# A macaron layer step in fp32: an inverse of corner blocks turned by TensorE in place of a round trip through DRAM, with sigmoid rewritten as tanh

## The chip, the cores and the metric

The kernel runs on one core of a Trainium2 chip. The metric is the device time of one execution in microseconds (us), the median of the runs. TensorE is PE in the profile (its weight loads are PEld), VectorE is DVE, ScalarE is ACT, GpSimd is POOL and SyncE is SP, which issues most DMAs.

## What is computed

One step of one layer, for 256 prompt tokens and 8 sample tokens, in fp32. The layer has three parts: a half-step SwiGLU FFN, mixing, and a second FFN, each behind an RMSNorm:

```python
x = x + FFN_RES * swiglu(rmsnorm(x, n1), f1g, f1u, f1d)
h = rmsnorm(x, nm)
proj = h @ w_in
...
o_att, k_buf, v_buf = attend(q, k, v, sinks)
o_rwkv, shift, S = rwkv_time_mix(proj[..., ATT_COLS:], ...)
mixed = jnp.concatenate([o_att, o_rwkv], axis=-1)
x = x + mixed @ w_out
x = x + FFN_RES * swiglu(rmsnorm(x, n2), f2g, f2u, f2d)
```

The change lies in `rwkv_time_mix` and, in two lines, in the softmax of the attention. For each head the state `S` (64 x 64) goes through the tokens:

```python
a = jax.nn.sigmoid(a0 + al @ a2)
g = jax.nn.sigmoid(gl) @ g2
kk = k * k_k
k = k * (1.0 + (a - 1.0) * k_a)
...
sa = einsum('bhij,bhj->bhi', S, -kk_t)
S = S * exp(lw_t)[:, :, None, :] + sa[..., None] * (kk_t * a_t)[:, :, None, :] + v_t[..., None] * k_t[:, :, None, :]
y_t = einsum('bhij,bhj->bhi', S, r_t)
```

## The kernel before

**Weights.** Every weight arrives from DRAM in pieces of 128 x 512 (`raw`, a ring of 6 buffers, issued by SP). ScalarE casts a piece to its high part (`hi`, line 123), VectorE subtracts for the low part (`lo`, through line 58), rings of 4 each. A piece makes twelve TensorE matmuls of 128 x 128 weights by 264 columns, three for each 128 x 128 block (`hi` with the two halves of x, `lo` with one), all recorded at line 74 as `acc<-s,hi` and `acc<-s,lo`. Both FFNs are little else.

**Mixing.** The input weights `win` (152 pieces) and the output weights `wout` go through the same path. After each piece `tick` lets every task, a Python generator, write one more stretch of its code, and `pause(n)` lets n pieces pass. The tasks are `prep` (one for each pair of heads, eight in all), `chain` (one for each batch of two pairs, four in all) and `attend` (one for each of eight query tiles). The scheduler of the language then puts the instructions of each engine in their final order, by a simulated timeline of its own. Each engine executes its queue in order.

**The chain of a batch.** RWKV runs in chunks of 64 tokens, four for each pair. `prep` computes the decay (`sg`, through sigmoid), `a`, the scaled keys `kr`, `bk`, and their masked products `gm` (`m<-kr,bk` on TensorE, the mask on VectorE). Each chunk needs the inverse of a triangular 64 x 64 matrix; its 32 x 32 corner blocks on the diagonal go by DMA to DRAM (`sa`) and return in two layouts, `X` and `Xt`, so that 128 partitions (4 column groups of 32 matrices) do the forward substitution: 30 steps on VectorE, each a product `st` and an addition to `Xt`. The result goes to DRAM once more (`sb`, line 544), returns as `TT` with a matrix to 32 partitions (line 549), VectorE adds the identity (line 556) and transposes (`TN`, line 559). From there: `TN,gm`, a copy `zs`, `TT,zs`, then `kr,TT`; the copies `W` (ScalarE) and `uv` (VectorE, line 596); `BT,W`, `gm,W`, `uv,BT`, `gm,uv`; `N` on VectorE; `N,PT` and the short chain over the four chunks; the group norm (`y,C`, `t,C`), the gate `sgl,ld`, and `mixed`, which the output weights take as their input.

`Xt`, `X`, `TN`, `zs` and `W` have one buffer, so the next batch's loads wait for the readers of this one. Small products use the five PSUM banks `m`, the big ones three `acc`. `DWAIT` and `PW` at the top of the file are the pauses.

Of the kernel before, what the change touches and what calls it, by code (L numbers as in the profile page):

```python
# [7 lines left out]
F32 = mybir.dt.float32  # L8
F32R = mybir.dt.float32r
AF = mybir.ActivationFunctionType  # L10
ALU = mybir.AluOpType
AX = mybir.AxisListType

P = 128
NP = 256
NB = 8
T = NP + NB
# [7 lines left out]
HALF = (slice(0, 64), slice(64, 128))  # L25
PARTS = [8, 7, 7, 7, 7, 7]
BATCH = [2, 2, 2, 2]
# [6 lines left out]
DWAIT = (8,8,8,4)  # L34
# [8 lines left out]
VMU, VKK, VKA, VA0, VRK, VLW, VLB, VSK, VSD = 64, 90, 98, 106, 114, 122, 130, 138, 154  # L43
# [4 lines left out]
def body(tc, I, O):  # L48
    nc = tc.nc
    V, A, G, TE, SP = nc.vector, nc.scalar, nc.gpsimd, nc.tensor, nc.sync  # L50
# [6 lines left out]
    def tt(e, out, a, b, op):  # L57
        return e.tensor_tensor(out=out, in0=a, in1=b, op=op)  # L58

    def stt(out, a, s, b, op0, op1):  # L60
        return V.scalar_tensor_tensor(out=out, in0=a, scalar=s, in1=b, op0=op0, op1=op1)  # L61

    def ts(e, out, a, s1, op0, s2=None, op1=None):
        k = {} if op1 is None else dict(op1=op1)
        e.tensor_scalar(out=out, in0=a, scalar1=s1, scalar2=s2, op0=op0, **k)

    def act(out, in_, f, **k):
        return A.activation(out=out, in_=in_, func=f, **k)  # L68

    def bc(ap, shape):  # L70
        return ap.broadcast_to(list(shape))

    def mm(out, lhsT, rhs, start=True, stop=True, **k):
        TE.matmul(out, lhsT, rhs, start=start, stop=stop, **k)  # L74
# [16 lines left out]
    def pause(n):  # L91
        for _ in range(n):
            yield

    with ExitStack() as ctx:
# [4 lines left out]
        dp = ctx.enter_context(tc.tile_pool(name="dp", bufs=1, space=bass.MemoryType.DRAM))  # L100
# [12 lines left out]
        def mp():  # L113
            return pp.tile([P, 512], F32, tag="m", bufs=NM, name=uid("m"))
# [28 lines left out]
        vec = cp.tile([P, NVEC], F32, name="vec")  # L143
# [13 lines left out]
        def vc(i):  # L157
            return vec[:, i:i + 1]
# [173 lines left out]
        def mixing_body(mx, n2, n3, XD):  # L332
            def fix(shape, name):
                return mx.tile(list(shape), F32, name=name)

            def ring(shape, tag, bufs):
                return mx.tile(list(shape), F32, tag=tag, bufs=bufs, name=uid(tag))
# [6 lines left out]
            ident, bo, cm = C[:, CID:CID + P], C[:, CBO:CBO + P], C[:, CCM:CCM + P]  # L344
# [7 lines left out]
            for pj in PJ:  # L352
                G.memset(pj[:, 0:1], 0.0)
            nmu = fix((P, NSH), "nmu")
            mu = vec[:, VMU:VMU + NSH]
            ts(V, nmu, mu, -1.0, ALU.mult, 1.0, ALU.add)
            tt(V, ss, ss, bc(mu.unsqueeze(2), (P, NSH, NB)), ALU.mult)
            qd = fix((P, 2, NB, 4), "qd")
            nbat = len(BATCH)
            scr = [dp.tile([BATCH[b] * 16, 1024], F32, tag=f"sa{b}", name=f"sa{b}") for b in range(nbat)]  # L360
            scr2 = [dp.tile([BATCH[b] * 16, 1024], F32, tag=f"sb{b}", name=f"sb{b}") for b in range(nbat)]
            mixed = [None] * 16
            have = [False]

# [19 lines left out]
            la, sgl = fix((P, T), "la"), fix((P, T), "sgl")  # L384
# [4 lines left out]
            def c4(x):  # L389
                return x[:, :NP].rearrange("p (c t) -> p c t", c=4)  # L390

            def prep(p, bt, k, xrr, xk, xv):
                lw = load(I["lw"][p], (P, 256))
                zp = mp()
# [3 lines left out]
                ap = mp()  # L398
                mm(ap[:, :T], lw[:, P:2 * P], la)
                sg, a = tmp(), tmp()  # L400
                act(sg, zp[:, :T], AF.Sigmoid)
                act(a, ap[:, :T], AF.Sigmoid, bias=vc(VA0 + p))
                kk, b = tmp(), tmp()
                act(kk, xk, AF.Copy, scale=vc(VKK + p))
                act(b, kk, AF.Square)
# [8 lines left out]
                W, Wi = tmp((P, 4, 65)), tmp((P, 4, 64))  # L414
# [5 lines left out]
                yield from pause(PW[1])  # L420
                rk = tmp((P, T + 2 * NB))
                stt(b, b, 1e24, kk, ALU.min, ALU.mult)
                tt(V, b, b, a, ALU.mult)
                ts(V, a, a, 1.0, ALU.subtract, vc(VKA + p), ALU.mult)
                kx = a
                stt(kx, a, 1.0, xk, ALU.add, ALU.mult)
                stt(rk[:, :T], xrr, vc(VRK + p), kx, ALU.mult, ALU.mult)
                yield
                BK, KR = ring((P, 4, 3, 64), "bk", 2), ring((P, 3, 4, 64), "kr", NKR)
                bt.KR[k] = KR  # L430
                stt(KR[:, 0], c4(kk), -1.0, W[:, :, 0:64], ALU.mult, ALU.mult)
                tt(V, KR[:, 1], c4(xrr), W[:, :, 1:65], ALU.mult)
                s4 = (P, 4, 2, 64)
                tt(V, BK[:, :, 0:3:2, :], bc(c4(b).unsqueeze(2), s4), bc(Wi.unsqueeze(2), s4), ALU.mult)
                tt(V, BK[:, :, 1, :], c4(kx), Wi, ALU.mult)
                for i, src in ((6, kk), (2, b), (3, xv), (4, kx), (5, xrr)):
                    G.tensor_copy(XD[:, i, p, :], src[:, NP:T])
                dq = rk[:, T:].rearrange("p (s b) -> p s b", s=2)
                tt(G, XD[:, 7, p, :], XD[:, 1, p, :], XD[:, 5, p, :], ALU.mult)
# [76 lines left out]
            def chain(bt):  # L516
# [24 lines left out]
                    if s % NSTEP == 0:  # L541
                        yield
                for g in range(ng):
                    SP.dma_start(scr2[bt.i].rearrange("r (j g t) -> g r j t", g=ng, t=32)[g], Y[g * nr:(g + 1) * nr])  # L544
                yield from pause(1)
                for h in range(2):
                    for blk in range(2):
                        x = h * 64 + blk * 32
                        SP.dma_start(TT[x:x + 32, :, blk * 32:blk * 32 + 32],
                                     scr2[bt.i].rearrange("(h b m) (s t) -> h b s m t", h=2, b=2, s=32)[h, blk])  # L550
                yield from pause(DWAIT[bt.i])
                for h in range(2):
                    for blk in range(2):
                        x = h * 64 + blk * 32
                        v = TT[x:x + 32, :, blk * 32:blk * 32 + 32]
                        tt(V, v, v, bc(ident[x:x + 32, x:x + 32].unsqueeze(1), (32, n * 4, 32)), ALU.add)
                TN = ring((P, n * 4, 32), "TN", 1)
                for h in range(2):
                    V.transpose(TN[h * 64:h * 64 + 32], TT[h * 64:h * 64 + 32, :, 0:32])
                yield  # L560
                ps = mp()
                for k in range(n):
# [29 lines left out]
                for k in range(n):  # L592
                    v = wus[k].rearrange("p (c t) -> p c t", c=4)
                    A.copy(W[:, k], v[:, 1:4, 0:64])
                    for h in range(2):
                        V.tensor_copy(uv[HALF[h], :, k, HALF[h]], v[HALF[h], :, 64:128])
                yield
                pbs = [mp() for _ in range(n)]
                for k in range(n):
# [101 lines left out]
            def softmax(s, mxv, sinks, n):  # L701
                nm, sm, es = (ring((P, 4), "st" + x, 6) for x in "abc")
                ts(V, nm[:, :n], mxv[:, :n], -1.0, ALU.mult)
                for j in range(n):
                    act(s[j], s[j], AF.Exp, bias=nm[:, j:j + 1], accum_out=sm[:, j:j + 1])
                w = n // len(sinks)
                for h, x in enumerate(sinks):
                    act(es[:, h * w:(h + 1) * w], nm[:, h * w:(h + 1) * w], AF.Exp, bias=x)
                tt(V, sm[:, :n], sm[:, :n], es[:, :n], ALU.add)
                V.reciprocal(sm[:, :n], sm[:, :n])  # L710
                for j in range(n):
                    ts(V, s[j], s[j], sm[:, j:j + 1], ALU.mult)

            def attend(t, q):
                p = t // 4
# [103 lines left out]
            shifted(0, la)  # L819
            act(tw[0:64, :], la[0:64, :], AF.Tanh)  # L820
            shifted(1, sgl)
            act(sgl, sgl, AF.Sigmoid)
            bat, att, bts = [], [], []
            for kind, i in SEQ:
                if kind == "b":
# [202 lines left out]
```

## Time and profile before

| | us |
|---|---|
| median of 3 runs | 2034.14 (2033.25 to 2035.09) |
| profiled execution | 2030.2, span 2028.1, clock 0.996 |
| mixing, by the trace | from about 796 to 1212 |
| TensorE busy in it | 396.25 of 416.50 |
| VectorE, ScalarE, POOL busy in it | 315.56, 233.94, 49.06 |

A row of the timeline has the start, the duration, the engine, the line, the operation, `out<-in`, shapes, and how many instructions it joins; the bracket is the engine's idle time before and what ended it. A window's row has, for each engine, its busy time in that stretch, then the granted clock, the DMA share and GB/s. An fp32 product shows as two matmul rows, so `x32` there is 16 products. A group's row has busy time and mean ns of one.

### The profile page before, as it was taken

How to read it: one execution, taken by the hardware profiler on the slowest of the kernel's cores; microseconds unless marked ns; L12 is line 12 of the kernel's file. 1: busy time of each engine (PE TensorE's matmuls, PEld its weight loads, DVE VectorE, ACT ScalarE, POOL GpSimd, SP SyncE). 2: the span in 40 equal slices, each digit the busy share in tenths (PEclk: the TensorE clock that was granted, in tenths of full speed). 3: DMA queues.
4: the chain of work that ended last, by engine and by line, in shares of the span. 5: the costliest groups of instructions: out<-in, count | busy, mean ns of one | idle time of the engine just before them, and what ended most of it. 6: DMA issues, size and time to landing. Idle time of an engine off the chain costs nothing.

```text
span 2028.1 us, 45390 instructions
## 1 busy us (share of the span) xinstructions
PE 1994.5 (98%) x17096; PEld 1956.8 (96%) x17096; DVE 1321.9 (65%) x2623; ACT 1035.2 (51%) x2027; POOL 240.9 (12%) x337
## 2 busy tenths in 40 slices
PE   9999999999999999999999899999999999999998
PEld 9999999999999999998898789999999999999998
DVE  5865555655556577678778766775666666666665
ACT  5644444444444466665555455554444444444445
POOL 0301001010110122111100010120101101010012
PEclk9999999999999999999999899999999999999999
DMA  6565655655556566554455345465566555655654
GB/s 226 178 187 196 184 193 188 185 185 176 186 170 192 181 207 204 155 159 121 134 148 166 91 133 185 171 184 178 191 181 195 180 192 189 187 191 180 195 181 145
DMA packets 227421, 358.38 MB, mean 177 GB/s; under 512 B 42353, under 2 KB 80769, under 8 KB 227201
## 3 DMA queue, kind: packets, MB, share of 16 engines
q1 hardware_dynamic: 220752, 346.95, 55.0%
q10 hardware_dynamic: 6448, 8.53, 1.3%
q8 instruction: 134, 2.20, 0.5%
q14 instruction: 87, 0.70, 0.1%
HBM read 347.25 MB, written 10.21 MB: 176 GB/s over the span
## 4 chain that ended last, share of the span: by engine, by line
PE 93%; DVE 3%; DMA 2%; ACT 1%; issue 1%; SPq 0%; ACTq 0%; DVEq 0%
PE acc L74 84%; PE m L74 7%; DVE lo L58 1%; DMA TT<-sb 1%; DMA sb<-Xt 0%; DMA raw<-in_win 0%; DVE y L58 0%; ACT t L68 0%; DVE t L678 0%; DMA raw<-in_gu 0%; DVE Xt L58 0%; DVE st L58 0%; ACT L68 0%; SPq L544 0%; DVE t L732 0%
## 5 line engine op out<-in xcount | busy, mean ns | idle before, releaser
L58 DVE TENSOR_TENSOR lo<-raw,hi 128x512 fp32r<-128x512 f32 (+1 forms) x1288 | 869.3, 679 | 546.4 <-ACT hi L123 518.5
L123 ACT CAST hi<-raw 128x512 fp32r<-128x512 f32 (+1 forms) x1288 | 775.9, 607 | 860.2 <-PE acc L74 777.6
L74 PE MATMUL acc<-s,hi 128*128 128x264 f32 x5940 | 1107.3, 286 | 4.7 <-ACT hi L123 2.5
L74 PEld LDWEIGHTS acc<-s,hi 128*128 128x128 f32 x5940 | 921.9, 188 | 10.3 <-issue 4.0
L74 PE MATMUL acc<-s,lo 128*128 128x264 f32 x2970 | 848.1, 286 | 5.3 <-DVE lo L58 5.3
L74 PEld LDWEIGHTS acc<-s,lo 128*128 128x128 f32 x2970 | 558.9, 188 | 8.8 <-DVE lo L58 6.6
L74 PE MATMUL acc<-t,hi 128*128 128x264 f32 x2752 | 503.0, 284 | 0.0
L74 PEld LDWEIGHTS acc<-t,hi 128*128 128x128 f32 x2752 | 426.3, 188 | 0.0
L74 PE MATMUL acc<-t,lo 128*128 128x264 f32 x1376 | 388.9, 285 | 0.0
L58 POOL TENSOR_TENSOR t<-t,t 128x264 f32<-128x264 f32 (+1 forms) x148 | 150.7, 1018 | 1151.2 <-ACT hi L123 791.0
L74 PEld LDWEIGHTS acc<-t,lo 128*128 128x128 f32 x1376 | 258.4, 188 | 0.1
L74 PE MATMUL acc<-y,hi 128*128 128x264 f32 x648 | 124.5, 284 | 0.0
L74 PEld LDWEIGHTS acc<-y,hi 128*128 128x128 f32 x648 | 101.8, 189 | 0.2
L74 PE MATMUL acc<-y,lo 128*128 128x264 f32 x324 | 92.5, 285 | 0.0
L58 DVE TENSOR_TENSOR t<-acc,t 128x264 f32<-128x264 f32 x156 | 67.4, 432 | 37.1 <-PE acc L74 36.9
L74 PE MATMUL acc<-o,hi 128*128 128x264 f32 x324 | 63.5, 286 | 0.0
L58 POOL TENSOR_TENSOR o<-o,o 128x264 f32<-128x264 f32 x43 | 35.9, 834 | 230.8 <-ACT o L68 225.1
L74 PEld LDWEIGHTS acc<-y,lo 128*128 128x128 f32 x324 | 60.8, 188 | 0.0
L61 DVE SCALAR_TENSOR_TENSOR s<-acc,s 128x264 f32<-128x264 f32 x96 | 40.6, 427 | 16.0 <-PE acc L74 15.5
L74 PEld LDWEIGHTS acc<-o,hi 128*128 128x128 f32 x324 | 50.3, 188 | 0.0
L74 PE MATMUL m<-s,hi 128*128 128x264 f32 x260 | 48.5, 285 | 0.0
L61 DVE SCALAR_TENSOR_TENSOR x<-acc,x 128x264 f32<-128x264 f32 x96 | 40.5, 427 | 10.0 <-PE acc L74 9.6
(236 smaller groups left out, 1288.7 us busy)
## 6 DMA issues: line engine op xcount, KB each, us to landing
raw<-in_gu SPq DMA_DIRECT2D x688, 256.0 KB, 3.3
raw<-in_dn SPq DMA_DIRECT2D x224, 256.0 KB, 2.8
raw<-in_win SPq DMA_DIRECT2D x152, 256.0 KB, 3.4
raw<-in_dn SPq DMA_DIRECT2D x160, 192.0 KB, 2.7
raw<-in_wout SPq DMA_DIRECT2D x64, 256.0 KB, 3.2
xsp<-x ACTq DMA_DIRECT2D x16, 132.0 KB, 3.2
s<-xsp SPq DMA_DIRECT2D x16, 132.0 KB, 4.2
ld<-in_sT SPq DMA_DIRECT2D x16, 128.0 KB, 3.2
```

What stands on the lines that cost most here:

```text
L58: return e.tensor_tensor(out=out, in0=a, in1=b, op=op)
L61: return V.scalar_tensor_tensor(out=out, in0=a, scalar=s, in1=b, op0=op0, op1=op1)
L74: TE.matmul(out, lhsT, rhs, start=start, stop=stop, **k)
L123: A.copy(hi[:, :w], raw[:, :w])
```

## The change

Four things are edited:

- The second trip through DRAM goes. POOL writes ones on the diagonal of `Xt`. 32 products with identity columns, `C,Xt`, bring the inverse on TensorE into one PSUM bank, 32 partitions for a matrix; ScalarE copies it to `TN`, and four VectorE transposes make `TT`. `TN,gm` reads the copy directly.
- Sigmoid becomes tanh of half the argument. Of `sg` and `sgl` POOL makes 0.5 t + 0.5; `a` stays a tanh, and its factor and offset go into the products that use it.
- Half of the `uv` copies, and two of four softmax scalings of an attention tile, go from VectorE to ScalarE.
- The pause behind the substitution is 8 pieces, in place of 1 and `DWAIT`.

```diff
+            half = fix((P, 16), "half")
+            ts(V, half, vec[:, VKA:VKA + 16], 0.5, ALU.mult)
+            less = fix((P, 8), "less")
+            ts(V, less, half[:, 0:8], -1.0, ALU.mult, 1.0, ALU.add)
...
-                act(sg, zp[:, :T], AF.Sigmoid)
-                act(a, ap[:, :T], AF.Sigmoid, bias=vc(VA0 + p))
+                act(sg, zp[:, :T], AF.Tanh, scale=0.5)
+                ts(G, sg, sg, 0.5, ALU.mult, 0.5, ALU.add)
+                act(a, ap[:, :T], AF.Tanh, scale=0.5, bias=half[:, 8 + p:9 + p])
...
-                tt(V, b, b, a, ALU.mult)
-                ts(V, a, a, 1.0, ALU.subtract, vc(VKA + p), ALU.mult)
+                stt(b, a, 1.0, b, ALU.add, ALU.mult)
+                act(a, a, AF.Identity, scale=half[:, p:p + 1], bias=less[:, p:p + 1])
                 kx = a
-                stt(kx, a, 1.0, xk, ALU.add, ALU.mult)
+                tt(V, kx, a, xk, ALU.mult)
...
-                stt(KR[:, 0], c4(kk), -1.0, W[:, :, 0:64], ALU.mult, ALU.mult)
+                stt(KR[:, 0], c4(kk), -0.5, W[:, :, 0:64], ALU.mult, ALU.mult)
...
-                for i, src in ((6, kk), (2, b), (3, xv), (4, kx), (5, xrr)):
+                ts(G, XD[:, 6, p, :], kk[:, NP:T], 0.5, ALU.mult)
+                for i, src in ((2, b), (3, xv), (4, kx), (5, xrr)):
...
                 for g in range(ng):
-                    SP.dma_start(scr2[bt.i].rearrange("r (j g t) -> g r j t", g=ng, t=32)[g], Y[g * nr:(g + 1) * nr])
-                yield from pause(1)
-                for h in range(2):
+                    G.memset(Y[g * nr:(g + 1) * nr].rearrange("p j t -> p (j t)")[:, g:g + (nj - 1) * (32 + ng) + 1:32 + ng], 1.0)
+                yield from pause(8)
+                ps = mp()
+                cols = ident[:, :ng * nr].rearrange("p (g h b m) -> p g h b m", g=ng, h=2, b=2)
+                for j in range(nj):
                     for blk in range(2):
+                        for h in range(2):
+                            x = h * 64 + blk * 32
+                            mm(ps[x:x + 32, j * ng * n * 4:(j + 1) * ng * n * 4], Y[:, j, :], cols[:ng * nr, :, h, blk, :])
+                TN = ring((P, n * 4, 32), "TN", 1)
+                A.copy(TN, ps[:, :32 * n * 4].rearrange("p (s m) -> p m s", m=n * 4))
+                yield
+                for blk in range(2):
+                    for h in range(2):
                         x = h * 64 + blk * 32
-                        SP.dma_start(TT[x:x + 32, :, blk * 32:blk * 32 + 32],
-                                     scr2[bt.i].rearrange("(h b m) (s t) -> h b s m t", h=2, b=2, s=32)[h, blk])
-                yield from pause(DWAIT[bt.i])
-                for h in range(2):
-                    for blk in range(2):
-                        x = h * 64 + blk * 32
-                        v = TT[x:x + 32, :, blk * 32:blk * 32 + 32]
-                        tt(V, v, v, bc(ident[x:x + 32, x:x + 32].unsqueeze(1), (32, n * 4, 32)), ALU.add)
-                TN = ring((P, n * 4, 32), "TN", 1)
-                for h in range(2):
-                    V.transpose(TN[h * 64:h * 64 + 32], TT[h * 64:h * 64 + 32, :, 0:32])
+                        V.transpose(TT[x:x + 32, :, blk * 32:blk * 32 + 32], TN[x:x + 32])
...
-                        V.tensor_copy(uv[HALF[h], :, k, HALF[h]], v[HALF[h], :, 64:128])
+                        (V.tensor_copy, A.copy)[h](uv[HALF[h], :, k, HALF[h]], v[HALF[h], :, 64:128])
...
-                    ts(V, s[j], s[j], sm[:, j:j + 1], ALU.mult)
+                    if j < 2:
+                        ts(V, s[j], s[j], sm[:, j:j + 1], ALU.mult)
+                    else:
+                        act(s[j], s[j], AF.Copy, scale=sm[:, j:j + 1])
...
-            act(sgl, sgl, AF.Sigmoid)
+            act(sgl, sgl, AF.Tanh, scale=0.5)
+            ts(G, sgl, sgl, 0.5, ALU.mult, 0.5, ALU.add)
```

The scheduler orders everything anew. In all, TensorE has 16227 instructions for 16099 (128 products more), VectorE 2587 for 2625, ScalarE 2077 for 2055 (with 16 table loads for 30), POOL 367 for 342, SP 1471 for 1503. Three places of the new order follow; the numbers behind a name tell buffers apart.

First, VectorE where the third batch's last `gm` pair ends (the second batch's inverse is being used then). Before:

```order
L58 TENSOR_TENSOR gm_13529<-m_13519,C 128x512
L58 TENSOR_TENSOR XD<-t_13361 128x8
L58 TENSOR_TENSOR gm_13551<-m_13520,C 128x512
L58 TENSOR_TENSOR lo_14432<-raw_14430,hi_14431 128x512
L58 TENSOR_TENSOR lo_14475<-raw_14473,hi_14474 128x512
L58 TENSOR_TENSOR lo_14497<-raw_14495,hi_14496 128x512
L58 TENSOR_TENSOR st_14050<-X_13624,Xt_13625 128x30
L58 TENSOR_TENSOR Xt_13625<-Xt_13625,st_14050 128x30
L58 TENSOR_TENSOR s_14427<-acc_14281,rs 128x264
```

Now:

```order
L58 TENSOR_TENSOR t_13392<-m_13504,t_13392 128x8
L58 TENSOR_TENSOR XD<-t_13392 128x8
L58 TENSOR_TENSOR gm_13560<-m_13550,C 128x512
L58 TENSOR_TENSOR gm_13582<-m_13551,C 128x512
L564 STREAM_TRANSPOSE TT_12606<-TN_13637 32x8x32 x4
L58 TENSOR_TENSOR st_14114<-X_13687,Xt_13688 128x30
L58 TENSOR_TENSOR Xt_13688<-Xt_13688,st_14114 128x30
L58 TENSOR_TENSOR st_14117<-X_13687,Xt_13688 128x29
```

Three `lo` stood between `gm` and the first `st`; now the four transposes of the second batch stand there.

Second, VectorE a little later, at the second batch's `uv` copies. Before:

```order
L58 TENSOR_TENSOR lo_14560<-raw_14558,hi_14559 128x512
L58 TENSOR_TENSOR st_14059<-X_13624,Xt_13625 128x27
L58 TENSOR_TENSOR Xt_13625<-Xt_13625,st_14059 128x27
L596 COPY uv_11356<-m_13758 64x4x64 x2
L58 TENSOR_TENSOR st_14111<-X_13624,Xt_13625 128x52
L58 TENSOR_TENSOR Xt_13625<-Xt_13625,st_14111 128x2x26
```

Now:

```order
L58 TENSOR_TENSOR lo_14425<-raw_14423,hi_14424 128x512
L58 TENSOR_TENSOR Xt_13688<-Xt_13688,st_14235 128x3x20
L58 TENSOR_TENSOR st_14238<-X_13687,Xt_13688 128x57
L58 TENSOR_TENSOR Xt_13688<-Xt_13688,st_14238 128x3x19
L601 COPY uv_11358<-m_13822 64x4x64
L58 TENSOR_TENSOR st_14271<-X_13687,Xt_13688 128x72
L58 TENSOR_TENSOR Xt_13688<-Xt_13688,st_14271 128x4x18
```

The first `uv` copy stood behind the fourth substitution step, counted by the widths of `st` (30, 29, 28, 27); now it stands behind the twelfth (30 down to 19 columns).

Third, TensorE near the end of mixing, at the last batch's gate `sgl,ld`. Before, with the pieces 168 to 170 (counted from the first of mixing) half done:

```order
L74 MATMUL m_15911<-t_15842,C 128x264
L74 MATMUL m_15916<-s_14555,o_15856 128x256
L74 MATMUL m_15916<-s_14555,o_15856 128x128
L74 MATMUL m_15917<-s_14555,o_15856 128x256
L74 MATMUL m_15917<-s_14555,o_15856 128x128
L74 MATMUL m_15965<-sgl,ld_15832 128x264
L74 MATMUL m_15969<-sgl,ld_15834 128x264
L739 MATMUL m_15991<-C,t_15498 128x128
```

Now, inside piece 163:

```order
L74 MATMUL acc_16837<-s_16428,hi_16839 128x264
L74 MATMUL m_16166<-s_14616,o_16106 128x256
L74 MATMUL m_16166<-s_14616,o_16106 128x128
L74 MATMUL m_16167<-s_14616,o_16106 128x256
L74 MATMUL m_16167<-s_14616,o_16106 128x128
L74 MATMUL m_16215<-sgl,ld_16082 128x264
L74 MATMUL acc_16837<-s_16429,hi_16839 128x264
L74 MATMUL acc_16837<-s_16428,lo_16840 128x264
```

The gate moved to an earlier piece, and its two products no longer stand together.

More of the change, by code (lines that the diff above doesn't have):

```diff
@@ L360, in mixing_body @@
             scr = [dp.tile([BATCH[b] * 16, 1024], F32, tag=f"sa{b}", name=f"sa{b}") for b in range(nbat)]
-            scr2 = [dp.tile([BATCH[b] * 16, 1024], F32, tag=f"sb{b}", name=f"sb{b}") for b in range(nbat)]
             mixed = [None] * 16
```

## The prediction

> **What bounds the kernel now.** I read the page's head first, then a table of windows by stage, then the timeline of TensorE wherever it shows idle time.
>
> ```profile
> span 2028.1 us, 45390 instructions
> PE 1994.5 (98%) x17096; PEld 1956.8 (96%) x17096; DVE 1321.9 (65%) x2623; ACT 1035.2 (51%) x2027; POOL 240.9 (12%) x337
> PE   9999999999999999999999899999999999999998
> PEclk9999999999999999999999899999999999999999
> core 0: us, PE busy (x) PEld busy (x) DVE busy (x) ACT busy (x) POOL busy (x), PEclk, DMA share, GB/s
> 70.00:770.00 700.00, 700.00 (x5758) 700.00 (x5758) 420.32 (x710) 342.60 (x619) 90.49 (x89) 1.00 0.59 188
> 898.00:976.90 78.90, 73.07 (x805) 68.28 (x803) 64.35 (x175) 42.87 (x98) 9.72 (x28) 1.00 0.48 136
> 976.90:1056.00 79.10, 74.46 (x828) 69.76 (x827) 60.61 (x170) 43.14 (x99) 7.50 (x22) 1.00 0.49 136
> 1056.00:1147.00 91.00, 86.08 (x1003) 77.12 (x1000) 70.55 (x229) 43.37 (x112) 4.63 (x8) 0.98 0.52 149
> 1147.00:1212.50 65.50, 60.68 (x412) 48.56 (x412) 42.38 (x137) 35.69 (x109) 6.67 (x18) 0.95 0.37 112
> ```
>
> TensorE is the bound: in the first FFN it is busy for 700.00 of 700 us, 121.6 ns per matmul (700/5758). The change touches only the mixing part, and there TensorE idles 78.90 - 73.07 = 5.83, 4.64, 4.92 and 4.82 us in the four windows, 20.2 in all. Two of them also ran below full clock: 2% of 91.00 and 5% of 65.50 are 1.8 and 3.3 us. So 25 us is all that a better order can give back; any added TensorE work is paid in full. VectorE's busy share there is not the limit, but it releases most of the waits:
>
> ```profile
> 916.16 0.33 PE L74 MATMUL m<-BT,W 64*64 64x64 f32 x4 [1.90 <-DVE uv L596]
> 917.53 1.15 PE L74 MATMUL m<-uv,BT 128*64 128x64 f32 x32 [0.46 <-DVE uv L596]
> 922.57 0.45 PE L74 MATMUL m<-N,PT 64*64 64x64 f32 x8 [0.55 <-DVE N L58]
> 965.59 0.39 PE L74 MATMUL acc<-s,lo 128*128 128x264 f32 x1 [1.26 <-DVE lo L58]
> 968.12 0.39 PE L74 MATMUL acc<-s,lo 128*128 128x264 f32 x1 [1.05 <-DVE lo L58]
> 993.26 0.33 PE L74 MATMUL m<-BT,W 64*64 64x64 f32 x4 [0.46 <-ACT W L594]
> 994.86 0.33 PE L74 MATMUL m<-BT,W 64*64 64x64 f32 x4 [0.69 <-DVE uv L596]
> 996.24 1.15 PE L74 MATMUL m<-uv,BT 128*64 128x64 f32 x32 [0.47 <-DVE uv L596]
> 1000.86 0.45 PE L74 MATMUL m<-N,PT 64*64 64x64 f32 x8 [0.63 <-DVE N L58]
> 1045.09 0.39 PE L74 MATMUL acc<-s,lo 128*128 128x264 f32 x1 [0.94 <-DVE lo L58]
> 1048.05 0.39 PE L74 MATMUL acc<-s,lo 128*128 128x264 f32 x1 [1.47 <-DVE lo L58]
> 1080.04 0.45 PE L74 MATMUL m<-N,PT 64*64 64x64 f32 x8 [0.94 <-DVE Xt L58]
> 1115.51 0.48 PE L74 MATMUL acc<-s,hi 128*128 128x264 f32 x2 [2.10 <-DVE s L58]
> 1116.59 0.39 PE L74 MATMUL acc<-s,lo 128*128 128x264 f32 x1 [0.60 <-DVE lo L58]
> 1149.37 1.16 PE L74 MATMUL m<-y,C 128*128 128x264 f32 x4 [1.36 <-ACT y L649]
> 1154.85 1.18 PE L74 MATMUL m<-s,o 64*128 64x256 f32 x8 [0.90 <-ACT t L68]
> 1158.93 1.25 PE L74 MATMUL m<-sgl,ld 128*128 128x264 f32 x2 [2.26 <-DVE mxv L732]
> ```
>
> The bracket is TensorE's idle time and who ended it. These waits come where VectorE itself had stood behind a transfer: its queue is in order, so whatever lies behind a waiting instruction (the `lo` halves of the weights, the `uv` copies) waits too.
>
> ```profile
> DVE TT L58 <- DMA TT<-sb: 13.2, 4, 4.3
> 976.89 0.44 PE L483 MATMUL m<-C,kr 128*128 128x128 f32 x2
> 978.68 0.68 DVE L58 TENSOR_TENSOR gm<-m,C 128x512 f32<-128x512 f32 x1
> 991.01 0.19 DVE L58 TENSOR_TENSOR st<-X,Xt 128x30 f32<-128x30 f32 x1 [3.55 <-DMA ld<-in_sT]
> 993.86 0.85 DVE L596 COPY uv<-m 64x256 f32<-64x256 f32 x2
> ```
>
> The first row says that VectorE stood 13.2 us in four waits for the inverse to come back from DRAM. The others give one batch's other round trip, which stays: from the end of `gm` (978.68 + 0.68 = 979.36) to the first substitution step `st` there are 11.65 us.
>
> **The change, part by part.**
>
> *Added products.* 128 products `C,Xt` (four batches of 32), each with 128 rows of weights by 32 columns and 32 moving columns. No such shape is in the trace. The nearest:
>
> ```profile
> 912.07 0.61 PE L74 MATMUL m<-C,t 128*128 128x128 f32 x4
> 912.44 0.37 PE L74 MATMUL acc<-s,lo 128*128 128x264 f32 x1
> 912.65 0.40 PE L74 MATMUL acc<-s,hi 128*128 128x264 f32 x2
> 918.48 0.72 PE L74 MATMUL m<-gm,uv 128*64 128x64 f32 x18
> 981.50 0.69 PE L74 MATMUL m<-TN,gm 32*32 32x32 f32 x32
> 982.12 0.71 PE L74 MATMUL m<-ld,tw 65*128 65x128 f32 x4
> ```
>
> A product of this type makes two rows of the trace. Starts give the pace: 16 products of 32x32 took 0.62 us (981.50 to 982.12), 39 ns each; 16 of 128 rows by 64 columns 0.95 us (917.53 to 918.48), 59 ns each; two of the full 128x128 0.37 us (912.07 to 912.44), 185 ns each. The new ones have the height of the second and the width of the first, so I take 50 ns, 6.4 us for all; the ends are 5.0 and 23.7 us, and the far end is unlikely since the 64-column row already has the full height. Nothing covers them.
>
> *Switches.* The first weight matmul after a group of small products takes 0.21 us (912.44 to 912.65), not 0.12. The new order has 26 more such changes in either direction: 26 x 0.09 = +2.3 us, between 0 (if only the large groups pay) and 4.7 (twice that). The page "TensorEngine Tiling (Array Packing)" of the Trainium skill, section "Key Properties", says that a change of tiling mode drains TensorE; the 0.09 us here agrees with a small drain, and it speaks against the change.
>
> *Taken away.* 32 DMAs and 16 identity additions on VectorE go, with the 13.2 us of waits; 16 small transposes replace 8 larger ones, 8 `uv` copies and 16 softmax scalings go to ScalarE, and one scaling per pair vanishes. ScalarE also loses tables, because sigmoid becomes tanh:
>
> ```profile
> L68 ACT ACT_TABLE_LOAD x21 | 26.9, 1283 | 4.5 <-PE m L74 4.2
> ```
>
> The program's loads fall from 30 to 16, 14 x 1.283 = 18 us of ScalarE, worth nothing directly: ScalarE is busy for 42.87 of 78.90 us, so the eight added copies and the scalings are covered too. POOL's new scalings and diagonal fills stand on an engine busy for a tenth; if it is late, the diagonal fill delays `C,Xt`, and `sg` behind it the products `m<-t,C`. I put both at 0, at most 2 us once. SP's queue loses 32 issues, but the next batch's `Xt` loads now wait for `C,Xt`, and the weight loads behind them with them; with six raw buffers I cost that at 0 (up to 2).
>
> What this does to the waits has to be walked stage by stage.
>
> *First inverse (window from 898).* `TN` no longer waits for DRAM, and `C,Xt` comes some nine weight pieces ahead of the `uv` copies. Of 1.90 + 0.46 + 0.55, with 0.60 more for `TN`, I leave 0.6 for `N`: -2.9 us.
>
> *Second (window from 976.9), the bad one.* Before, three `lo` stood on VectorE between `gm` and the next batch's `st`, and only four substitution pairs between that and the `uv` copies. Now no `lo` stands in that gap, the pieces of the chain come earlier on TensorE, and the first `uv` copy stands behind twelve pairs and three `lo`. From the end of the `kr,bk` products (976.89): `gm` ends and `st` starts 14.1 us later, as now, perhaps 0.6 sooner since one weight issue less lies between the loads; a pair takes about 0.45 us (993.86 less 991.01 holds four with other work) and a `lo` 0.6, so twelve and three are 7.2 us, and two more pairs and the copies end the second `uv` at 22.8. TensorE gets there sooner than now: 46 weight matmuls (5.6 us) in place of 72 (8.8), the other products as now, 7.1 us, and 1.6 for `C,Xt`, 14.3 us to `BT,W` and 1.4 more to `uv,BT`. It waits 22.8 - 15.7 = 7 us (4 if the pairs run without gaps, 9 if the load is late), then 0.8 for `N`. After such a gap the clock falls:
>
> ```profile
> 1150.00:1175.00 25.00, 21.55 (x114) 14.48 (x113) 16.77 (x61) 14.46 (x42) 1.80 (x4) 0.86 0.15 46
> ```
>
> In this window the granted clock was 0.86, so 25 x 0.14 = 3.5 us were lost after idle gaps of 0.90 and 2.26 us; half that, 1.7, I charge here. The page "TensorE: Matmul & The Clock Gate" of the Trainium skill, section "What's actually happening", puts TensorE at half clock after an idle window of about 3.4 us; the forecast gap of 7 us holds one or two, and by it the loss would be 1.7 to 3.4 us. Against this stand the waits it replaces, 0.46 + 0.69 + 0.47 + 0.63 = 2.25, and the 1.26 + 1.05 of `lo`, which go with the lighter VectorE. Sum: 7 + 0.8 + 1.7 - 4.6 = +4.9.
>
> *Third (window from 1056).* Three `lo` stay between the `gm` and `st`. Of 0.94 + 1.47 + 0.94, with 0.26 for `uv`, I keep 1.3: -2.3.
>
> *Fourth and the end.* The last inverse no longer passes DRAM, and its products stand some ten weight pieces earlier, the gate (`sgl,ld`) about five. Now 2.10 + 0.60 and 1.36 + 0.90 + 2.26, with 1.8 + 3.3 of clock, make 12.3. `mixed` of the last pair still ends a chain, and the attention heads now stand among its products; I keep 4.3 us: -8, between -3 and -11.
>
> **Sum.** 6.4 + 2.3 - 2.9 + 4.9 - 2.3 - 8 = +0.4 us. The profiled execution took 2030.2 us (2028.1 of span), 3.9 below the median of 2034.14; by the median, which is what counts, the sum gives 2034.5. Since the stage that costs most is also the most uncertain downward (an early load cuts it, nothing shows it above 9), I say 2033.5.
>
> **Rivals.** 0.2% of the time, 4 us, is what a measurement tells from no change.
>
> *Faster:* in the second stage the next batch's `st` finds its data early, or `uv` comes before TensorE gets there. Then the 7 and the 1.7 go: 2034.5 - 8.7 = 2025.8. For it speaks that VectorE has 2 us less to do per pair; against it the 11.65 us from `gm` to `st`, which the change doesn't shorten. It decides once that wait is under some 3 us.
>
> *Slower:* the waits only change hands. TensorE now waits for VectorE's last `Xt` and ScalarE's copy in its own queue, where formerly the DMA was waited for by VectorE alone; then the gains of the first, third and last stage (13.2) halve, to 6.6, and the time is 2034.5 + 6.6 = 2041. It decides where the end gives back under 4 us. The waits 0.94 behind `Xt` and 2.26 behind `mxv` speak for it; that the products stand many pieces before their users, against it.
>
> *Products dear:* at 185 ns they cost 17.3 us more, 2052. The 59 ns of the 128-row products speak against it.
>
> **Chances.** The forecast (within 2029 to 2038) 0.45, faster rival 0.27, slower rival 0.23, dear products 0.05. Of the forecast's 0.45 about 0.08 lies beyond -4 us and 0.02 beyond +4: faster 0.35, same 0.37, slower 0.28 (the small rest of the rivals lies inside). The range runs from 2023 (below the faster rival by a few us, for a bigger gain at the end) to 2044 (above the slower, for a stall of 9 and two half-clock windows); it leaves out the dear products and the tails.
>
> **What would show it.** A group `C,Xt` of 256 rows with a pace near 50 ns; no `TT<-sb`; near the second batch's `uv,BT` a single gap of 4 to 9 us in TensorE's timeline, with VectorE before it waiting for the load behind `gm`, and a stretch of half clock; no waits of `lo` near 965 and 1045; in the last window less idle time than 4.8 us and a clock above 0.95. I am wrong if that gap is missing or doubled, if a wait for `Xt` or for `TN` stands ahead of the products, or if the last window is no better.

## The result and the profile after

The changed kernel takes 2023.32 us (median of 4 runs, 2021.17 to 2025.77), the kernel before 2034.62 beside it: 0.9934 times as long [0.9911, 0.9956], 11.3 us less by the medians and 13.4 by the ratio. The profiled execution of the changed kernel was its longest, 2025.77 us; that of before, 2030.2, was shorter than all runs of before beside it (2033.25 to 2035.76). The two traces therefore show 4.4 us of difference.

The head of the page after:

```profile
span 2024.0 us, 45924 instructions
PE 1999.5 (99%) x17352; PEld 1967.0 (97%) x17352; DVE 1310.7 (65%) x2585; ACT 1033.0 (51%) x2049; POOL 252.5 (12%) x362
PE   9999999999999999999899999999999999999998
PEclk9999999999999999999999989999999999999999
```

TensorE is busy 5 us more (1999.5 for 1994.5) in a span 4 us shorter. The dent in its row of digits moved from the last stage of mixing to the second inverse. The windows by stage, as before:

```profile
898.00:976.90 78.90, 77.36 (x972) 72.21 (x973) 60.23 (x166) 48.67 (x123) 14.41 (x38) 1.00 0.47 131
976.90:1056.00 79.10, 73.32 (x885) 68.90 (x885) 58.24 (x159) 40.90 (x100) 9.52 (x24) 0.96 0.47 128
1056.00:1147.00 91.00, 87.36 (x986) 77.65 (x982) 68.44 (x229) 51.70 (x143) 4.56 (x12) 0.96 0.48 139
1147.00:1212.50 65.50, 65.27 (x453) 58.41 (x450) 40.81 (x119) 33.47 (x91) 7.26 (x18) 0.87 0.43 131
```

Idle time of TensorE is 1.54, 5.78, 3.64 and 0.23 us, for 5.83, 4.64, 4.92 and 4.82 before. In the last window it is gone, yet the clock fell from 0.95 to 0.87. TensorE's timeline, at every wait that is left, and at the second batch's new products:

```profile
914.00 0.33 PE L74 MATMUL m<-BT,W 64*64 64x64 f32 x4 [1.45 <-ACT W L599]
966.80 1.16 PE L74 MATMUL m<-kr,bk 64*128 64x128 f32 x16
967.89 0.76 PE L74 MATMUL m<-C,Xt 128*32 128x32 f32 x64
968.59 0.44 PE L488 MATMUL m<-C,kr 128*128 128x128 f32 x2
988.42 0.48 PE L74 MATMUL m<-BT,W 64*64 64x64 f32 x4 [5.78 <-ACT W L599]
1062.42 0.48 PE L74 MATMUL m<-BT,W 64*64 64x64 f32 x4 [3.32 <-ACT W L599]
1109.38 0.97 PE L74 MATMUL m<-t,s 128*64 128x128 f32 x4 [0.22 <-DVE t L751]
1152.55 0.48 PE L74 MATMUL acc<-s,hi 128*128 128x264 f32 x2 [0.23 <-DVE s L58]
```

From 898 us on twenty-one waits (places where TensorE is idle for 0.15 us or more: the seventeen shown in the prediction and four others) became five, and no `lo` is among them. The 32 products `C,Xt` run from 967.89 to 968.59: 0.70 us, 22 ns each. The long wait stands where the forecast put it, and its cause is in VectorE's and ScalarE's timelines and the table of waits (sum, count, longest); the two rows of TensorE show what ran behind it:

```profile
967.99 1.29 DVE L58 TENSOR_TENSOR gm<-m,C 128x512 f32<-128x512 f32 x2 [0.16 <-PE m L74]
980.02 0.19 DVE L58 TENSOR_TENSOR st<-X,Xt 128x30 f32<-128x30 f32 x1 [9.03 <-DMA Xt<-sa]
987.22 0.41 DVE L601 COPY uv<-m 64x256 f32<-64x256 f32 x1
979.16 0.32 ACT L599 COPY W<-m 128x192 f32<-128x192 f32 x1 [1.02 <-PE m L74]
987.66 0.37 ACT L601 COPY uv<-m 64x256 f32<-64x256 f32 x1 [8.18 <-DVE uv L601]
988.05 0.32 ACT L599 COPY W<-m 128x192 f32<-128x192 f32 x1
989.90 1.97 PE L74 MATMUL m<-uv,BT 128*64 128x64 f32 x32
991.65 1.55 PE L74 MATMUL m<-gm,uv 128*64 128x64 f32 x32
ACT uv L601 <- DVE uv L601: 18.7, 7, 8.2
```

VectorE waits 9.03 us for the next batch's load, then does substitution steps until its `uv` copy at 987.22. ScalarE's half of the `uv` copies, which reads the same product and writes the same tile as VectorE's, waits 8.18 us for it, and the second `W`, which needs nothing from VectorE, stands behind it in ScalarE's queue. `BT,W` follows at 988.42.

### The profile page after: what moved, and what is told of

It is laid out like the page before. It is cut to its first block, busy times and chain, and to the rows that moved or that the text cites. A ratio compares the mean times of both kernels' runs of the same rounds, so it can differ in the third digit from the quotient of the medians.

```text
span 2024.0 us, 45924 instructions
## 1 busy us (share of the span) xinstructions
PE 1999.5 (99%) x17352; PEld 1967.0 (97%) x17352; DVE 1310.7 (65%) x2585; ACT 1033.0 (51%) x2049; POOL 252.5 (12%) x362
## 4 chain that ended last, share of the span: by engine, by line
PE 96%; DVE 2%; DMA 1%; issue 0%; ACT 0%; SPq 0%; DVEq 0%; ACTq 0%
PE acc L74 87%; PE m L74 9%; DMA raw<-in_gu 1%; DVE lo L58 0%; DVE y L58 0%; PE m L501 0%; DVE Xt L58 0%; DVE st L58 0%; ACT t L68 0%; SPq L534 0%; DMA Xt<-sa 0%; SPq L533 0%; PE m L747 0%; PE m L449 0%; DMA s<-xsp 0%
```

## What half clock and a wait really cost

Where the clock was low is in these rows (windows of the changed kernel, and TensorE's 8-column products of the decode, `m<-t,ld`, from its timeline):

```profile
986.90:996.90 10.00, 8.48 (x128) 8.08 (x129) 9.79 (x30) 4.70 (x13) 3.70 (x5) 0.71 0.18 47
1169.82 2.74 PE L74 MATMUL m<-t,ld 128*128 128x8 f32 x24
1166.00:1173.00 7.00, 7.00 (x61) 6.75 (x60) 5.15 (x16) 5.10 (x17) 0.00 (x0) 1.00 0.61 177
1173.00:1181.00 8.00, 8.00 (x43) 8.00 (x42) 3.20 (x9) 2.88 (x7) 0.00 (x0) 0.57 0.63 186
1181.00:1190.00 9.00, 9.00 (x79) 8.29 (x78) 6.18 (x20) 4.25 (x10) 0.00 (x0) 1.00 0.44 135
1190.57 2.74 PE L74 MATMUL m<-t,ld 128*128 128x8 f32 x24
1194.00:1205.00 11.00, 11.00 (x53) 9.39 (x52) 4.52 (x12) 3.74 (x11) 2.91 (x10) 0.53 0.13 40
```

At the wait at 988 the clock is halved for 6.8 us (from 985.8 in the clock's records), at the one at 1062 for 6.8 us more (from 1060.9). In the last window it is halved twice, for 6.8 and 10.2 us, with TensorE busy for 8.00 of 8.00 and 11.00 of 11.00 us: no idle time precedes it, but each time a group of 24 rows of 8-column products does. The page "TensorE: Matmul & The Clock Gate" of the Trainium skill, section "What's actually happening", ties half clock to an idle window of about 3.4 us; the stretches here are all multiples of 3.4 us, and the one at the 5.78 us wait agrees. The one at 1060.9 does not: TensorE had then been idle for 1.8 us only (the 3.32 us wait begins at 1059.10). Those of the last window came without idle time.

To size both, I took the distance between successive starts of TensorE's matmuls in the two traces, between the same two weight matmuls (from 790.04 to 1305.82 us before, 515.8 us; from 790.84 to 1302.31 after, 511.5). Each distance is compared with the mean for the same two kinds of neighbours at full clock and without idle time, over ten of the traces. What a distance has above that mean is a wait where the timeline shows idle time, and else, where the clock is halved, loss by half clock. From one weight matmul to the next it is 127 ns at full clock and 227 at half; between rows of the 128x64 products `uv,BT` 32 and 54; between rows of the 8-column products 100 and 192. These are estimates from the rows. By the stages of the prediction (in us, waits + loss by half clock):

| stage | before | after | measured | forecast |
|---|---|---|---|---|
| first inverse | 3.8 | 1.6 | -2.2 | -2.9 |
| second, with the two `lo` at 965 | 5.2 | 5.9 + 1.8 | +2.6 | +4.9 |
| third, with the two `lo` at 1045 | 4.1 | 3.5 + 2.4 | +1.7 | -2.3 |
| fourth and end | 9.2 + 4.0 | 1.0 + 7.7 | -4.5 | -8 |
| ahead of 898 | 0 | 1.0 | +1.0 | 0 |
| products | | 128 x 22 ns | +2.8 | +6.4 |
| switches | | 13 more each way | +1.9 | +2.3 |
| all other matmuls at full clock | | | -7.6 | 0 |
| sum | | | -4.3 | +0.4 |

In all, waits fell by 9.3 us and the loss by half clock rose by 7.9 (from 4.0 to 11.9). The row ahead of 898 is one `lo` wait that the forecast did not have. The last row but one is what remains of the 4.3 us: 4.9 of it stands at places where one kind of small product follows another (393 in place of 417), 2.7 among small products of one kind, which follow one another more closely. What makes them closer is not shown.

Two readings of the page need care. A bracket is a little shorter than what its removal saves: the brackets of the twenty-one waits of before add up to 19.9 us, their starts stand 22.3 us further apart than normal, 0.1 us more for each. And the window's clock counts too much: 15.3 us by (1 - clock) x window after, where half clock took 11.9, since a stretch that falls on idle time costs nothing. What it falls on behind the wait pays: the 32 rows `uv,BT` took 1.75 us to the next group (989.90 to 991.65), for 0.95 at full clock before (917.53 to 918.48), and the whole stretch lost 1.8 us.

## Experiments

Five kernels came out below every range expected of them (inverse only, products twice, pauses 10, 7 and 12); `uv` all on ScalarE and two fillers came out above what the tested cause would give, and one filler between its two ranges. Each ratio is to runs of before made beside that kernel on the same chip. Those medians of before lie between 2031.8 and 2034.7, so differences between two kernels below are given by the ratios, or by both where they differ.

| kernel | median, us | ratio to before |
|---|---|---|
| whole change | 2023.32 | 0.9934 [0.9911, 0.9956] |
| inverse only | 2017.85 | 0.9926 [0.9909, 0.9942] |
| rest only, DRAM kept | 2026.29 | 0.9963 [0.9951, 0.9975] |
| copies and scalings only | 2029.05 | 0.9979 [0.9969, 0.9988] |
| inverse and tanh | 2018.46 | 0.9925 [0.9905, 0.9946] |
| products twice | 2012.96 | 0.9896 [0.9873, 0.9919] |
| one filler | 2021.15 | 0.9943 [0.9923, 0.9962] |
| two fillers | 2025.57 | 0.9954 [0.9939, 0.9969] |
| fewer decode products | 2012.30 | 0.9891 [0.9876, 0.9906] |
| `uv` all on ScalarE | 2019.06 | 0.9921 [0.9906, 0.9935] |
| pause 7 | 2007.14 | 0.9874 [0.9855, 0.9893] |
| pause 10 | 2003.15 | 0.9856 [0.9834, 0.9877] |
| pause 12 | 2001.90 | 0.9839 [0.9825, 0.9854] |
| inverse only, pause 10 | 2008.42 | 0.9872 [0.9855, 0.9888] |
| before, later steps | 2031.20 | 0.9983 [0.9968, 0.9998] |

**Which part does it.** First the hunks of the inverse alone (products in place of DRAM, pause 8), then all the others with the DRAM trip kept, then of these only the two moves to ScalarE:

```diff
-                        V.tensor_copy(uv[HALF[h], :, k, HALF[h]], v[HALF[h], :, 64:128])
+                        (V.tensor_copy, A.copy)[h](uv[HALF[h], :, k, HALF[h]], v[HALF[h], :, 64:128])
...
-                    ts(V, s[j], s[j], sm[:, j:j + 1], ALU.mult)
+                    if j < 2:
+                        ts(V, s[j], s[j], sm[:, j:j + 1], ALU.mult)
+                    else:
+                        act(s[j], s[j], AF.Copy, scale=sm[:, j:j + 1])
```

> Only the inverse by TensorE (products with identity columns, pause of 8), sigmoid and the engines of the copies as before. Theory A (the gain is the second DRAM trip, behind which VectorE stood 13.2 us and TensorE's waits at lo, uv and the tail): most of the gain, 2023 to 2027 us. Theory B (the gain is the lighter VectorE and ScalarE: tanh, moved copies): 2031 to 2036, since the products cost 3 to 6 us and the waits only change hands.

> Everything but the inverse: tanh in place of sigmoid, half of the uv copies and two of four softmax scalings on ScalarE; the inverse by DRAM as before. Theory A: 2031 to 2036, the four waits for TT<-sb stay at about 13 us. Theory B: 2022 to 2028.

> Only the copies and scalings moved from VectorE to ScalarE; every engine's order is otherwise that of before. Theory A: 2032 to 2036. Theory B: 2027 to 2031. A third possibility: slower by 1 to 4 us, because ScalarE's uv copy waits for VectorE's and holds the W copy behind it, as the 5.78 us wait of the changed kernel shows.

By the ratios the inverse alone gives 15.0 us, the rest alone 7.5, the copies 4.3 of them. 15.0 + 7.5 is not the whole change's 13.4 (at most 18.1 by its interval): the parts do not add, because each sets another order. The inverse alone has a long wait too, but in the third stage, and the last window has none at all:

```profile
1052.66 0.48 PE L74 MATMUL m<-BT,W 64*64 64x64 f32 x4 [3.35 <-ACT W L593]
1147.00:1212.50 65.50, 65.50 (x516) 59.85 (x515) 45.77 (x122) 34.06 (x87) 7.05 (x18) 1.00 0.50 156
```

With the DRAM trip kept, its waits stay, though at 8.4 us and not the 13 expected (the first row is from the table of waits), and the time still falls:

```profile
DVE TT L58 <- DMA TT<-sb: 8.4, 6, 2.7
1109.18 0.24 PE L74 MATMUL m<-TN,gm 32*32 32x32 f32 x2 [2.52 <-DVE TN L565]
```

The tanh part added to the inverse, without the moves:

> The inverse by TensorE and tanh for sigmoid, without the copies moved to ScalarE. If the moved copies are what makes the whole slower than the inverse alone (2023.3 against 2017.9 us): 2013 to 2018 us. If tanh is: 2020 to 2025. If only the order counts (here two lo and five steps at the second inverse, one lo and seventeen steps at the third): a short wait at the second, one over 5 us with half clock at the third, 2016 to 2023 us.

It changes nothing beside the inverse alone. So at this pause the moves to ScalarE, good for 4.3 us by themselves, give nothing on top, and perhaps take some back (0.9925 to 0.9934, 2018.46 to 2023.32; the intervals overlap). All `uv` copies on ScalarE, so that none waits for VectorE's half, tests the wait behind that:

```diff
-                        (V.tensor_copy, A.copy)[h](uv[HALF[h], :, k, HALF[h]], v[HALF[h], :, 64:128])
+                        A.copy(uv[HALF[h], :, k, HALF[h]], v[HALF[h], :, 64:128])
```

> The whole change, pause 8, with all uv copies on ScalarE instead of half. If the waits at BT,W and uv,BT come from the uv copies standing behind the substitution on VectorE, both waits (5.8 and 3.3 us) shrink under 1.5 us, at most a wait at lo takes their place: 2005 to 2014 us. If ScalarE then is the late one (its hi behind the copies): waits at hi, 2015 to 2024.

0.9921 for 0.9934, the intervals overlap. In its trace the second inverse's `BT,W` comes without a wait, but that of the third, which was to shrink under 1.5 us too, is 4.00 us long. ScalarE's wait for VectorE's half is shown in the trace of the change; what it alone costs is not settled.

**What the products cost.** The line `mm(ps[x:x + 32, ...` of the inverse is written twice:

> Each of the 128 products C,Xt written twice, to the same place. Price: 22 ns a product, as the trace of the changed kernel shows (2.8 us for 256 rows), gives +2.8 us of TensorE; 50 ns, the forecast's, +6.4; 185 ns +24. The order shifts with it (one lo, seven steps at the second inverse), so the time of the group of 64 in a batch is read from the trace: 1.4 us against 3.2. In all 2015 to 2026 us.

```profile
967.67 1.48 PE L74 MATMUL m<-C,Xt 128*32 128x32 f32 x128
969.08 0.44 PE L488 MATMUL m<-C,kr 128*128 128x128 f32 x2
```

64 products take 1.41 us, again 22 ns each: 2.8 us more of work. Yet the kernel is 8 us faster by the ratios (10 by the medians) than with them once, since its order came out with waits of 1.71, 1.86 and 1.33 us for `BT,W` in place of 5.78 and 3.32. A repetition prices an operation by its rows, not by the total, where a scheduler reorders.

**The order.** `pause(8)` becomes 10, 7 and 12 in the whole change, 10 in the inverse alone, and in the kernel before the pauses ahead of the inverse's use grow by two (`DWAIT` of 10, 10, 10, 6 for 8, 8, 8, 4):

```diff
-                yield from pause(8)
+                yield from pause(10)
```

> The whole change with a pause of 10 pieces instead of 8 before the products; the scheduler then leaves three lo between the third batch's gm and its first st, and six substitution steps (not twelve) before the second batch's uv copies. Theory A (the 5.8 and 3.3 us waits at BT,W and the half-clock stretches after them come from VectorE standing behind the load with uv and lo behind it): no wait over 2 us at the second inverse, no half clock near 986, 9 us or more come back: 2010 to 2017 us. Rival (the wait is for TensorE's own chain, or half clock falls at random): 2021 to 2026 us.

> The whole change with a pause of 7 pieces: three lo between gm and st in the second and third places, five steps before uv in both. Theory A: as with 10, 2010 to 2018 us, less sure since C,Xt comes one piece nearer to the last substitution step and may wait for it (under 1.5 us). Rival: 2021 to 2026 us.

> Only the inverse by TensorE, as in the first experiment, with the pause of 10. It says what tanh and the moved copies are worth once no long wait is left. Theory A (with good order TensorE is nearly always busy, so lighter VectorE and ScalarE add little): 2003 to 2008 us. Theory B (they matter by themselves, 4 to 7 us as they did on the kernel before): 2008 to 2014.

> The kernel before with its DRAM trip, DWAIT at 10, 10, 10, 6 in place of 8, 8, 8, 4: the control for the pause. If the gain of the pause of 10 is one of order alone, this also falls, by 5 to 20 us, to 2012 to 2028. If the DRAM trip is what keeps VectorE standing, it stays within 2028 to 2038 us, some waits for TT<-sb shorter, the last chain later.

> The whole change with a pause of 12. If 10 already takes every wait away, the same within 2 us at the inverses, with the last chain two pieces later: 2002 to 2008 us; if the last batch then ends too late for the output weights, a wait in the last window and 2006 to 2014.

Pause 10 is 16 us faster than 8 by the ratios, 20 by the medians, with the same work. Two of its windows, and the second inverse there on TensorE and VectorE:

```profile
976.90:1056.00 79.10, 79.08 (x1044) 73.77 (x1040) 66.85 (x213) 42.08 (x105) 10.36 (x23) 1.00 0.46 131
1147.00:1212.50 65.50, 65.50 (x543) 63.10 (x543) 43.83 (x92) 32.76 (x73) 4.54 (x12) 1.00 0.55 163
979.98 0.33 PE L74 MATMUL m<-BT,W 64*64 64x64 f32 x4
960.00 1.28 DVE L58 TENSOR_TENSOR gm<-m,C 128x512 f32<-128x512 f32 x2
971.61 0.19 DVE L58 TENSOR_TENSOR st<-X,Xt 128x30 f32<-128x30 f32 x1 [2.50 <-DMA Xt<-sa]
980.10 0.41 DVE L601 COPY uv<-m 64x256 f32<-64x256 f32 x1
```

The load and the copy are no earlier: from the end of `gm` (961.28) to `st` 10.3 us, to `uv` 18.8, for 10.7 and 17.9 at pause 8. TensorE comes later, with 83 weight matmuls on the way in place of 46: `BT,W` 18.7 us behind `gm`, where at pause 8 TensorE was ready after 13.4 (988.42 less the 5.78 of waiting, less 969.28). So the wait is filled with weight matmuls. Sized as above, over the same stretch of weight matmuls, the trace with 10 is 20.5 us shorter than that with 8: 8.5 of waits (13.0 to 4.5) and 11.9 of half clock (7.7 of it in the last window), which is gone from mixing here. All the rest together differs by 0.1, so these two account for the gain. Since pause 7 is almost as good (0.9874), it is not lateness as such that counts: at 8 the order is a bad one. For before later pauses hardly count (0.9983); its trace then has one wait of 9.47 us for `TN`, with `TT<-sb` still there:

```profile
1119.39 0.31 PE L74 MATMUL m<-TN,gm 32*32 32x32 f32 x2 [9.47 <-DVE TN L559]
DVE TT L58 <- DMA TT<-sb: 11.1, 4, 5.0
```

So later use alone, in the one setting tried, does not replace what the products do. At pause 10 the rest of the change saves 3.3 us on top of the inverse by the ratios (intervals overlap). Pause 12 is the fastest version found, 0.9839, some 33 us below before, though the prediction held that a better order can give back 25 at most; it and 10 are not told apart.

**The half clock of the last window.** Behind each decode product stands one filler, a weight-like product of 264 columns whose result nobody reads (`z` is a tile of `mixed`), or two of them. The cut shows the helper's product for one filler and one of its two calls:

```diff
+                    mm(bank[:, P:P + T], z[:, 0:P], z)
...
                             mm(sv[:, :, c0:c0 + 4], kc[:, j, :], qb[:, p, b + j])
+                            filler(sps)
```

> The changed kernel, with one full-size fp32r matmul (128 x 264, its result unused) beside each of the 32 decode-attention products of 8 columns (m<-t,ld). Theory C (the half clock between 1173 and 1204 follows from these products keeping TensorE nearly empty without any idle time): the clock stays full there, 8 us come back, the fillers cost 2 to 4: 2016 to 2020 us, and the runs scatter less. Rival (the half clock there comes from the earlier waits or at random): the same dips, and 2024 to 2028 us, slower by the fillers.

> The changed kernel with two products of 264 columns (some 0.12 us each by the first filler run's rows) put behind each of the decode's 8-column products; VectorE's order unchanged, the result the same. Theory: no half clock in the last window, granted clock 0.995 or more, 2018 to 2022 us though TensorE has some 10 us more to do. Rival: the dips stay and the fillers only add; 2025 to 2032 us.

> The changed kernel with the decode's products (m<-t,ld, 8 columns each) replaced by a few of 16 columns, most of them left out (the decode's result is not computed); VectorE's order unchanged. Theory (the runs of 8-column products draw the half clock of the last window, two stretches of 17 us together in the changed kernel's profile): no half clock between 1166 and 1210 us, the one after the second inverse stays; about 2010 us (2005 to 2013), of which some 5 us are the products themselves. Rival (the dips there come from elsewhere, as the wait 100 us earlier or the power of the whole): dips stay in the last window; 2015 to 2019 us, by the products alone.

With one filler one of the two half-clock stretches stayed in the profiled execution, and the runs spread from 2016.8 to 2026.0: not settled by that. With two fillers, and with most of the products left out, none was left in the last window; these are the windows of the two kernels, in this order, where the change had its second stretch and 53 matmuls:

```profile
1194.00:1205.00 11.00, 11.00 (x82) 9.22 (x81) 8.07 (x17) 5.81 (x15) 4.29 (x12) 1.00 0.16 49
1194.00:1205.00 11.00, 11.00 (x92) 11.00 (x92) 7.57 (x15) 6.10 (x12) 0.00 (x0) 1.00 0.53 159
```

The second inverse's wait is still there in the latter (5.84 us), so the products and not that wait draw the half clock of this order. Leaving most of them out gives 8.7 us by the ratios, 11.0 by the medians: 20 products less are 4.4 at 0.22 each, and with the 7.7 of half clock it would be 12.1. Two fillers cost 7.8 us by their rows (0.47 us for a product with them, 0.22 without, 32 times), so less 7.7 the time should be that of the change. Between the profiled executions it is 0.6 us more, by the medians 2.3 and by the ratios 4.1, above what the theory expected. The clock came out as expected (0.995 or 0.996 in all five runs), the time did not; the medians' part of it is not settled.

The same groups do nothing in the kernel with pause 10:

```profile
1148.28 2.74 PE L74 MATMUL m<-t,ld 128*128 128x8 f32 x24
1148.00:1158.00 10.00, 10.00 (x90) 9.50 (x89) 5.70 (x16) 5.39 (x16) 0.00 (x0) 1.00 0.64 193
```

The same group, the same length, and the clock stays at 1.00. The clock's records show what separates them. In each of the sixteen traces the clock changes only at the edges of steps of 3.41 us, and where the steps lie differs from trace to trace (the remainder of an edge's time by 3.41 is 0.86 us in before, 2.77 in the change, 2.61 with pause 10, 0.50 with pause 12). A group of 24 rows lasts 2.7 us. In the change 2.4 us of the first and all of the second lie within one step (1170.13 to 1173.54, 1190.61 to 1194.02), and the half clock begins at that step's end; with pause 10 an edge at 1149.49 cuts the group at 1148.28 into 1.2 and 1.5. The thirteen traces with all decode products and no filler have 24 groups of 24 rows without a long gap. Eight of them have 2.4 us or more within one step, and half clock follows at its end each time; sixteen have 2.14 us or less, and it never does. So which groups draw half clock goes with how they fall into these steps. No run moved the steps on purpose, and no choice in the kernel is seen to place them: for the change, two such hits in the profiled execution are bad luck, and pause 10 had good luck there.

## Why the prediction missed

It said no change within what can be measured, 2033.5; the kernel became 11.3 us faster, at the low edge of the range (2023). The steps that failed are the median, which was taken to lie as far above the trace as before's, and in the sum the terms for TensorE's own work; the waits and the clock, for which most of the working was done, came out worse than forecast, not better. The table by stages above has the sizes.

- *Sum and median*: the traces' own sum is -4.3, and the forecast added the offset of before's profiled execution (+3.9) to the changed kernel as if both executions stood alike to their medians. Before's was 4.4 under, the changed kernel's 2.5 over: 6.9 of the 11.3 us are in neither trace. A part goes with the clock, so with how much half clock an execution drew: the change's two runs at 0.991 took 2025.77 and 2024.90, those at 0.992 and 0.993 2021.73 and 2021.17, and before's runs beside the experiments average 2032.3 at 0.996, which was the clock of before's profiled execution, and 2034.4 at 0.994. That is some 2 us of before's 4.4 and the 2.5 of the change; the rest is open.
- *Added products*, mis-sized: 22 ns each, below the lower end of 39 ns that the 32x32 products had suggested, let alone the 50 taken. +2.8 for +6.4.
- *Switches*: +1.9 for +2.3, as forecast. But they were the only term for TensorE's other work, and the rest of it, put at nothing without a reason, gave back 7.6, the largest miss of the sum. Its cause stays open.
- *First inverse, `TT<-sb`, the `lo` waits*: as forecast, -2.2 for -2.9.
- *Second inverse*: place and mechanism were right (`st` 10.7 us after `gm`, `uv` behind twelve pairs and three `lo`, a wait of 5.78 us for the 7 forecast, half clock of 1.8 for the 1.7 charged). `N` did not wait, and what the long wait replaced was worth 5.2 and not 4.6. +2.6 for +4.9.
- *Third stage*: waits of 1.3 were kept, 3.5 are left, since `BT,W` waits 3.32 us for `W` there too, and half clock takes 2.4 more. +1.7 for -2.3. The *slower rival* had named ScalarE's copy standing in its own queue; it is the releaser of all three large waits.
- *Fourth and end*: the waits went as said, more than said (9.2 to 1.0). What took most of it back was not a wait but half clock without idle time, 7.7 us, where 4.3 had been kept for waits and clock together. -4.5 for -8.

Waits and clock of all stages gave -1.4 for -8.3; the products and the other matmuls at full clock gave -2.9 for +8.7. That the sum came near zero, as forecast, is these two cancelling, so luck. The *faster rival* had nearly the right time (2025.8) for the wrong reason: the second wait did not go.

## What to carry to other kernels

Price half clock by the matmuls that it falls on and not by the window's mean: here a weight matmul paid 100 ns, a row of an 8-column product 92, a row of a 128x64 product 22, and only idle time paid nothing. Compare such distances kind by kind: a mean over all small products hides the loss, since those behind the wait are among the shortest (32 ns a row for `uv,BT` at full clock, 56 over all). Where one long wait replaces several short ones, sum both sides in the same measure before calling it a loss. Where a scheduler orders the code, a change's parts do not add and one pause is one draw: try a few neighbouring values before judging the change, here worth as much (16 us and more) as the change itself (13).

## What the hardware showed unexpectedly

- Half clock without idle time: 6.8 and 10.2 us behind groups of twelve 8-column products (2.74 us each), TensorE busy throughout; gone when the products were filled up or left out. The clock changed only at the edges of 3.41 us steps, and of 24 such groups the eight with 2.4 us or more in one step drew half clock, the sixteen with 2.14 or less did not.
- An fp32 product of 128 rows by 32 columns with 32 moving columns, in four column groups in turn, took 22 ns; one of 32x32 had 39 ns, one of 128 rows by 64 columns 59 ns.
